# A two-layer state-space and attention trunk: the last state-space round to the end in order of use, the norm multiplied in with the scale, forget gates in steps between the value tiles, heads' loads on SyncE's queue

## The chip, the cores and the metric

The kernel runs on one core of one Trainium2 chip. The core has a matmul engine (PE, with weight loads PEld), a vector engine (DVE), an activation engine (ACT), a general engine (POOL) and SyncE (SP), which here only issues DMAs. Each engine works through its own row of instructions in order and waits on semaphores for the others; a DMA that POOL or SP issues stands in that engine's row too. The metric is device time in microseconds (us), the median of the runs. A profile of one execution, with a trace of every instruction, comes with it.

## The reference

One sequence of 1024 tokens, width 1024, passes two layers, all in float32. Shift, scale and gate of each sub-layer come from a conditioning vector c.

```python
h = _rms(x, a_norm_g) * (1 + scale) + shift            # layer 0: S5
u, z = split(h @ w_in, 2)
s = linear_scan(u)                                      # 64 groups of 16, 64 complex states
y = gelu(C @ s + D * u)
y = y * sigmoid(y @ w_glu + b_glu) * silu(z)
x = x + gate * (y @ w_out)

h = _rms(x, kv_g) * (1 + scale) + shift                 # shared keys, values, forget gates
k, v, f = split(h @ kv_w)
k = _head_rms(k, k_g);  F = cumsum(log_sigmoid(f + f_bias))

h = _rms(x, b_g) * (1 + scale) + shift                  # layer 1: attention with decay
q, z = split(h @ w_in, 2);  q = _head_rms(q, q_g) / 8
p = softmax(q @ k.T + F_i - F_j, causal)
x = x + gate * (((p @ v) * silu(z)) @ w_out)
```

## The kernel before

Every matrix product is computed from a high and a low part of both factors: `act[0]`, `act[1]` (tiles aH, aL) and `w_hi`, `w_lo`, in three matmuls (high by high, low by high, high by low). ACT makes the high part by a copy, DVE (now and then POOL) the low part by a subtraction. `weight_strip` (L83) loads 128 columns of a weight into the only `w_raw` buffer and splits them. The activations lie with the features on partitions; the 1024 tokens are two halves of 512.

The stages, with the time where each begins in the profile:

- 0 to 295 us: projections u and z, and the S5 rounds e = 0 to 7. PE's steps of a round are interleaved by hand with matmuls of the z strips, of 512, 256 or 258 columns, which `unit(n)` hands out. The last round calls `unit(2)` (L699) before `states_out`, which reads the scanned and rotated states r (L639); `unit(99)` hands out the rest.
- 295 to 387: GLU. For tile (e, i), `zt` and `yt` are loaded, `project` (L113) makes 24 matmuls into one of the two PSUM buffers of pool `pj`, and ACT's sigmoid `sg` (L772) reads it.
- 387 to 488: the out projection, 16 tiles in the order OUT_SEQ: (6,0), (7,0), (6,1), (7,1), (4,1), (5,1) are the last. Each ends in x1 = x + gate * y (L796, DVE), a store of x1 by POOL, a square (ACT) and a sum of squares (L804, POOL). After the last tile of a half, matmuls with ones give the mean, and `neg2_rsqrt` (L163) makes q2x from it: ACT Identity, Ln, Exp, then three operations of DVE.
- Norm and modulation for keys and values (L831 to 835): x1 is multiplied by q2x in place, even k on DVE and odd k on POOL, then `modulated` (L172) scales and shifts on ACT (aH) and DVE (hmod) and subtracts (aL).
- to 810: six jobs of token tiles, v0, v2, k0, k2, q0, q2 (L932). A token tile is 24 matmuls (tkps, L861) of 128 tokens by 256 columns, 272 in v0, into one of three PSUM buffers of pool `psa`. A job takes, for each half i, two strips d of four tiles. A value tile is split into vt and stored by SP; v0 also copies the forget gates' columns to flog (L875). A key or query tile goes ACT hsq (L885), DVE reduce hms (L886), POOL hms (L887, L888), DVE hnt (L890); four hnt are transposed on PE into trps (L897), split to kh and kl and stored by SP. `forget_gates` stands between v0 and v2. The second layer's activations (`modulated` with s_b, sh_b, L944) stand before q0 in the program and may be issued once k0 is done.
- 810 to 1132: attention, 64 steps of two query blocks; scores are made LOOK = 2 steps ahead. `head` (L989) loads a head's kk, qs, q and vhl, two buffers each. Between steps PE is handed matmuls of the z strips (zb) and of the first rows of the final projection (f), Z_STEP items a step, Z_END in the last.
- 1132 to the end: the other rows of the final projection (pj_f).

Between them, 64 products with the modulation weights ("gemv", modw, L131) run on DVE; `mod_load` (L136) issues the load of the next, and `mod_take` (L145) the product.

What sets the order: the framework schedules with a timing model of its own, engine by engine, in which `tc.issue_after(x)` adds an edge. What it decides is the fixed row of each engine.

```python
Q.dma_start(...)   # SP's row        G.dma_start(...)   # POOL's row
T = PE, V = DVE, S = ACT, G = POOL
```

Of the kernel before, what the change touches and what calls it, by code (L numbers as in the profile page):

```python
# [20 lines left out]
P = 128  # L21
# [16 lines left out]
F_ROWS, Z_END = 2, 2  # L38
# [7 lines left out]
def trunk(tc, a, out):  # L46
# [3 lines left out]
    with top:  # L50
# [30 lines left out]

        def weight_strip(src, shape, l_eng=None, pool=None):
            raw = (pool or wpool).tile(shape, F32, name="w_raw", tag="w_raw", bufs=2 if pool else 1)  # L83
            Q.dma_start(out=raw, in_=src)
            hi = wpool.tile(shape, F32R, name="w_hi", tag="w_hi")
            lo = wpool.tile(shape, F32R, name="w_lo", tag="w_lo")
            split(raw, hi, lo, None, l_eng)
            return hi, lo

        def copy_on(eng, o, i):  # L90
            if eng is S:
                S.activation(o, i, AF.Copy)  # L92
# [5 lines left out]
        def split(x, hi, lo, h_eng=None, l_eng=None):  # L98
            copy_on(h_eng or S, hi, x)
            (l_eng or V).tensor_tensor(out=lo, in0=x, in1=hi.bitcast(F32), op=ALU.subtract)  # L100
# [7 lines left out]
        def project_part(ps, w, act, half, ks, k0=0, k1=KT - 1):  # L108
            for k in ks:
                for n, (wt, at) in enumerate(((0, 0), (0, 1), (1, 0))):  # L110
                    T.matmul(ps, w[wt][:, k, :], act[at][k][half], start=(k == k0 and n == 0), stop=(k == k1 and n == 2))  # L111

        def project(w, act, half, nm):  # L113
            ps = pj.tile([P, HL], F32, name="pj_" + nm, tag="pj")
            project_part(ps, w, act, half, range(KT))
            return ps
# [19 lines left out]
        def mod_load(behind):  # L136
            n = mod_next[0]
            if n < 64:
# [24 lines left out]
        def neg2_rsqrt(v, r, ps, o):  # L163
            S.activation(v, ps, AF.Identity, bias=eps_t)
            S.activation(r, v, AF.Ln)
            S.activation(r, r, AF.Exp, scale=-0.5)
            V.tensor_tensor(out=v, in0=v, in1=r, op=ALU.mult)
# [4 lines left out]
        def modulated(x, k, i, s, sh, act, pool=None, l_eng=None):  # L172
            sl = slice(HL * i, HL * i + HL)
            h = pool.tile([P, HL], F32, name="hmod", tag="hmod", bufs=2) if pool else x[k][:, sl]
            S.activation(act[0][k][i], x[k][:, sl], AF.Identity, scale=s[:, k:k + 1], bias=sh[:, k:k + 1])
            V.tensor_scalar(out=h, in0=x[k][:, sl], scalar1=s[:, k:k + 1], scalar2=sh[:, k:k + 1], op0=ALU.mult, op1=ALU.add)
            (l_eng or V).tensor_tensor(out=act[1][k][i], in0=h, in1=act[0][k][i].bitcast(F32), op=ALU.subtract)  # L177
# [14 lines left out]
        with l0:  # L192
# [487 lines left out]
            for e in range(KT):  # L680
# [17 lines left out]
                if e % 2 == 0 or not more:  # L698
                    unit(1 if more else 2)  # L699
# [41 lines left out]
        x1 = [xnp.tile([P, L], F32, name=f"x1_{k}", tag=f"x1_{k}") for k in range(KT)]  # L741
        l0b = ExitStack()
        wvx = ExitStack()
        with l0b:
# [6 lines left out]
            yt = [yp.tile([P, TC, NCH], F32, name=f"yt{k}", tag=f"yt{k}") for k in range(KT)]  # L751
            for e, i in [(e, i) for e in range(KT - 2) for i in range(2)] + [(e, i) for i in range(2) for e in (KT - 2, KT - 1)]:
# [6 lines left out]
                with tc.issue_after(last_y):  # L759
                    last_q = Q.dma_start(out=zt, in_=z_d[P * e:P * e + P, i]).ins  # L760
                    if i == 0:
                        last_q = Q.dma_start(out=yt[e], in_=y_rows(e)).ins
# [7 lines left out]
                if e:  # L770
                    ps = project(wg[e], act, i, f"g{e}_{i}")
# [10 lines left out]
            psa = top.enter_context(tc.tile_pool(name="psa", bufs=3, space=PSUM, side="right", reuse_waits="tile"))  # L782
            psb = top.enter_context(tc.tile_pool(name="psb", bufs=3, space=PSUM, side="right", reuse_waits="tile"))
            gate_a = mod_bias(16, 24, "gate_a")
            held, acc, seen = {}, [None] * 2, [0, 0]
            for e, i in OUT_SEQ:
                sl = slice(HL * i, HL * i + HL)
                if e not in held:
                    if len(held) == 2:
                        del held[min(held, key=lambda n: held[n][0])]  # L790
                    held[e] = (len(seen) + sum(seen), weight_strip(a["a_w_out"][e], [P, KT, P], V, wk))
                xr = wk.tile([P, HL], F32, name="xr", tag="zt2")
                xd = Q.dma_start(out=xr, in_=a["xT"][:, e, sl]).ins
                mod_load(xd)
                ps = project(held[e][1], act, i, f"o{e}_{i}")
                mod_take(V.scalar_tensor_tensor(out=kj(x1[e][:, sl]), in0=jk(ps), scalar=gate_a[:, e:e + 1], in1=kj(xr),  # L796
                                                op0=ALU.mult, op1=ALU.add).ins, 2)
# [7 lines left out]
                else:  # L805
# [3 lines left out]
                    mps = pj.tile([P, HL], F32, name=f"ms1_{i}", tag="pj")  # L809
                    T.matmul(mps, onesm, acc[i], start=True, stop=False)  # L810
                    T.matmul(mps, onesm, sq, start=False, stop=True)
# [427 lines left out]
```

## Time and profile before

| what | us |
|---|---|
| median of 3 runs | 1207.44 (1205.32 to 1210.37) |
| the profiled execution | 1206.17 |
| its span in the trace | 1204.4 |
| PE busy / weight loads | 1153.0 / 1020.9 |
| DVE / ACT / POOL busy | 854.5 / 606.3 / 376.0 |

The profile is of one execution. "Idle before, releaser" is the time an engine stood before an instruction, and the instruction whose end let it go on. In the rows of the timeline the columns are start, duration, engine, line, operation, output <- inputs, shapes, count, and in brackets the idle time before. A q behind an engine's name marks its queue of DMAs. The granted clock is the share of PE's full clock that the throttle let through.

The costliest group of PE is the token tiles' matmul, and that of DVE the split of the transposed probabilities:

```profile
L861 PE MATMUL tkps<-wvh,aH 128*128 128x256 f32 (+1 forms) x768 | 220.6, 288 | 5.5 <-DVE flog L875 4.8
...
L1068 DVE TENSOR_TENSOR ptl<-tp,pth 128x512 fp32r<-128x512 f32 (+1 forms) x192 | 101.2, 552 | 10.6 <-ACT pth L1067 10.1
```

Such a row has the group's count, its busy time in us, the mean of one in ns, and the idle time ahead of it.

### The profile page before, as it was taken

Reading aid. Unit: us, or ns where it says so; the run is one execution under the profiler, and the core shown is the slowest. Engines: PE = TensorE matmul, PEld = TensorE weight load, DVE = VectorE, ACT = ScalarE, POOL = GpSimd, SP = SyncE. Lnnn points to the kernel's source line nnn. Section 1 sums busy time; section 2 is a strip of 40 time slices with the busy share of each in tenths; the row PEclk is TensorE's granted clock in tenths of the full one; section 3 lists DMA queues with packets and bytes.
Section 4 is the critical chain, followed back from the end, with each engine's and each line's share of the span. In section 5 each row is a group of like instructions: output and inputs, shape, how many; then the busy total and the mean of one; then the engine's idle time right before and its main releaser. Section 6 shows DMA issues by size and latency. Waiting matters only on the chain.

```text
span 1204.4 us, 20401 instructions
## 1 busy us (share of the span) xinstructions
PE 1153.0 (96%) x7414; PEld 1020.9 (85%) x7414; DVE 854.5 (71%) x1725; ACT 606.3 (50%) x1140; POOL 376.0 (31%) x586
## 2 busy tenths in 40 slices
PE   8989998997999998899999999999999999999898
PEld 6879887886788786889999989998888898888686
DVE  7889899885399877875444664347888788887421
ACT  6666766665335234322223443237677777885310
POOL 4000000000000234510044483437576665764100
PEclk9999999998999999999999999999999999999999
DMA  9754556584976894467524275527696978951342
GB/s 359 222 175 128 164 167 163 158 218 151 328 231 192 281 324 140 148 190 248 179 74 173 106 143 165 131 84 151 102 157 112 136 118 112 155 92 27 100 162 79
DMA packets 110388, 197.09 MB, mean 164 GB/s; under 512 B 17136, under 2 KB 58224, under 8 KB 108752
## 3 DMA queue, kind: packets, MB, share of 16 engines
q1 hardware_dynamic: 83072, 153.25, 40.3%
q0 software_dynamic: 25216, 37.76, 19.4%
q10 hardware_dynamic: 2000, 4.79, 1.6%
q8 instruction: 59, 0.97, 0.4%
q14 instruction: 41, 0.34, 0.1%
HBM read 138.21 MB, written 46.27 MB: 153 GB/s over the span
## 4 chain that ended last, share of the span: by engine, by line
PE 67%; DVE 13%; ACT 8%; DMA 4%; issue 4%; POOL 2%; SPq 1%; ACTq 0%; POOLq 0%; DVEq 0%
PE tkps L861 17%; PE u L274 7%; PE pj_o L111 6%; PE pj_f L111 6%; PE zb L111 5%; PE pj_g L111 5%; PE tp L1065 4%; PE ov L1072 3%; PE ov L1071 3%; PE sp L1033 2%; PE sp L1034 2%; PE z L274 2%; DVE r L207 1%; DVE w_lo L100 1%; PE f L111 1%
## 5 line engine op out<-in xcount | busy, mean ns | idle before, releaser
L861 PE MATMUL tkps<-wvh,aH 128*128 128x256 f32 (+1 forms) x768 | 220.6, 288 | 5.5 <-DVE flog L875 4.8
L861 PE MATMUL tkps<-wvl,aH 128*128 128x256 f32 (+1 forms) x768 | 217.3, 284 | 0.0
L861 PE MATMUL tkps<-wvh,aL 128*128 128x256 f32 (+1 forms) x768 | 217.0, 283 | 0.2 <-POOL aL L177 0.2
L861 PEld LDWEIGHTS tkps<-wvh,aH 128*128 128x128 f32 x768 | 145.9, 190 | 6.9 <-issue 5.4
L861 PEld LDWEIGHTS tkps<-wvl,aH 128*128 128x128 f32 x768 | 146.0, 190 | 0.3 <-issue 0.2
L861 PEld LDWEIGHTS tkps<-wvh,aL 128*128 128x128 f32 x768 | 145.5, 190 | 0.7 <-POOL aL L177 0.4
L1067 ACT ACTIVATE pth<-tp 128x512 fp32r<-128x512 f32 (+1 forms) x192 | 87.0, 488 | 56.8 <-PE ov L1071 30.6
L1040 ACT ACTIVATE pr<-pr,mx 128x128 f32<-128x128 f32 (+7 forms) x128 | 98.8, 773 | 22.6 <-DVE mx L1037 21.1
L1042 POOL TENSOR_SCALAR pr<-pr,sm 128x128 f32<-128x128 f32 (+7 forms) x128 | 95.9, 758 | 43.5 <-DVE sm L1041 41.5
L1068 DVE TENSOR_TENSOR ptl<-tp,pth 128x512 fp32r<-128x512 f32 (+1 forms) x192 | 101.2, 552 | 10.6 <-ACT pth L1067 10.1
L92 ACT ACTIVATE w_hi<-w_raw 128x1024 fp32r<-128x1024 f32 x49 | 51.6, 1054 | 90.5 <-PE pj_f L111 29.1
L1037 DVE CUSTOM_DVE_ANT_0 pr<-sp,msk 128x512 f32<-128x512 f32 (+3 forms) x128 | 72.7, 569 | 23.8 <-PE tp L1065 21.0
L1071 PE MATMUL ov<-pth,vhl 128*128 128x256 f32 x320 | 85.8, 300 | 0.2
L1065 PE MATMUL tp<-ident,pr 128*128 128x128 f32 x576 | 84.2, 275 | 1.1 <-DVE ptl L1068 1.0
L885 ACT ACTIVATE hsq<-tkps 128x256 f32<-128x256 f32 x64 | 24.5, 383 | 116.2 <-PE tkps L861 111.0
L1072 PE MATMUL ov<-ptl,vhl 128*128 128x256 f32 x320 | 81.0, 286 | 0.2
L1065 PEld LDWEIGHTS tp<-ident,pr 128*128 128x128 f32 x576 | 69.3, 141 | 11.5 <-DVE ptl L1068 2.7
L1033 PE MATMUL sp<-kk,qs 128*128 128x256 f32 (+2 forms) x192 | 71.5, 375 | 2.8 <-DVE mx L1037 2.4
L888 POOL TENSOR_TENSOR hms<-hms,nhalf 128x4 f32<-128x4 f32 x64 | 68.7, 1074 | 5.0
L890 DVE TENSOR_TENSOR hnt<-tkps,hms 128x256 f32<-128x256 f32 x64 | 27.0, 422 | 60.2 <-POOL hms L888 60.1
L1034 PE MATMUL sp<-kk,q 66*128 66x256 f32 (+2 forms) x192 | 66.2, 348 | 0.0
L887 POOL TENSOR_SCALAR hms<-hms 128x4 f32<-128x4 f32 x64 | 13.0, 203 | 165.2 <-DVE hms L886 164.1
(328 smaller groups left out, 3264.0 us busy)
## 6 DMA issues: line engine op xcount, KB each, us to landing
modw<-modw SPq DMA_DIRECT2D x48, 512.0 KB
wvr<-kvq_w SPq DMA_DIRECT2D x12, 1024.0 KB
mwx<-modw SPq DMA_DIRECT2D x16, 512.0 KB
w_raw<-a_w_in SPq DMA_DIRECT2D x16, 512.0 KB
v_d<-vt SPq DMA_DIRECT2D x32, 256.0 KB
kk<-k_d POOLq DMA_DIRECT2D x16, 512.0 KB, 7.6
vhl<-v_d POOLq DMA_DIRECT2D x16, 512.0 KB, 8.6
qs<-q_d POOLq DMA_DIRECT2D x32, 256.0 KB, 5.1
```

Of the source, the lines that this page charges most:

```text
L111: T.matmul(ps, w[wt][:, k, :], act[at][k][half], start=(k == k0 and n == 0), stop=(k == k1 and n == 2))
L274: m = T.matmul(ps[:, 0:c1 - c0], w[wt][:, k, :], act[at][k][i][:, c0:c1], start=(k == 0 and n == 0), stop=(k == KT - 1 and n == 2)).ins
L861: T.matmul(ps[:, 0:nv], at, wt[:, k, 0:nv], start=(n == 0), stop=(n == 3 * KT - 1))
L1033: T.matmul(sp[:, 0:wm_], qsl, kk[:, 0, lo:lo + wm_], start=True, stop=False)
L1034: T.matmul(sp[:, 0:wm_], q1_[:, P * i:P * i + P], kk[0:HD + 2, 1, lo:lo + wm_], start=False, stop=True)
L1040: S.activation(pr[:, 0:nk], pr[:, 0:nk], AF.Exp, scale=-1.0, bias=mx, accum_out=sm)
L1042: G.tensor_scalar(out=pr[:, 0:nk], in0=pr[:, 0:nk], scalar1=sm, scalar2=0.0, op0=ALU.mult, op1=ALU.add)
L1065: T.transpose(out=tp[:, b, :], in_=prs[qi][:, P * (b0 + b):P * (b0 + b) + P], identity=ident)
L1067: S.activation(pth[:, 0:m, dst], tp[:, 0:m, :], AF.Copy)
L1068: V.tensor_tensor(out=ptl[:, 0:m, dst], in0=tp[:, 0:m, :], in1=pth[:, 0:m, dst].bitcast(F32), op=ALU.subtract)
L1071: T.matmul(ov, vhl[:, b, :], pth[:, b - b0, :], start=(b == 0), stop=False)
L1072: end = T.matmul(ov, vhl[:, b, :], ptl[:, b - b0, :], start=False, stop=(b == nb - 1)).ins
```

## The change

1. The last S5 round calls `unit(3)`.
2. GLU and out tiles take their PSUM buffers from `psa` (three), which is opened earlier; the loads of zt and yt are chained in order of use.
3. `mod_load` stops at the 40th product until v2; the other 24 are loaded and taken in v2, k0 and k2. `mod_take` in the out stage keeps one held.
4. `neg2_rsqrt` has no Identity pass. `modulated` multiplies x1 by scale and q2x in one operation (DVE), adds the shift on ACT (aH) and in the subtraction (aL, DVE). The passes on x1 of L834 go, and POOL's share of the low parts. The mean of half 0 is put between the halves of the next out tile; half 1 of the keys' and values' modulation is put between the tiles of v0.
5. Value stores move from SP to POOL; vt takes the buffers of kh and kl. The forget gates are a generator, advanced between the tiles of v2.
6. The z strips' generator stands ahead of the jobs, and its first eight items are issued in q2's last half.
7. `head` issues all loads on SP.
8. F_ROWS is 3 and Z_END 4; row 2's strip wf2 lies in a buffer of kk.

```diff
-F_ROWS, Z_END = 2, 2
+F_ROWS, Z_END = 3, 4
...
-        def project(w, act, half, nm):
-            ps = pj.tile([P, HL], F32, name="pj_" + nm, tag="pj")
-            project_part(ps, w, act, half, range(KT))
+        def project(w, act, half, nm, pool=None, tag="pj", between=None):
+            ps = (pool or pj).tile([P, HL], F32, name="pj_" + nm, tag=tag)
+            m = project_part(ps, w, act, half, range(KT // 2))
+            if between:
+                with tc.issue_after(m):
+                    m = between()
+                with tc.issue_after(m):
+                    project_part(ps, w, act, half, range(KT // 2, KT))
+            else:
+                project_part(ps, w, act, half, range(KT // 2, KT))
             return ps
...
-        def mod_load(behind):
+        def mod_load(behind, end=5 * KT):
             n = mod_next[0]
-            if n < 64:
+            if n < end:
...
         def neg2_rsqrt(v, r, ps, o):
-            S.activation(v, ps, AF.Identity, bias=eps_t)
-            S.activation(r, v, AF.Ln)
+            S.activation(r, ps, AF.Ln, bias=eps_t)
             S.activation(r, r, AF.Exp, scale=-0.5)
-            V.tensor_tensor(out=v, in0=v, in1=r, op=ALU.mult)
+            V.scalar_tensor_tensor(out=v, in0=ps, scalar=EPS, in1=r, op0=ALU.add, op1=ALU.mult)
...
-        def modulated(x, k, i, s, sh, act, pool=None, l_eng=None):
+        def modulated(x, k, i, s, sh, act, pool=None):
...
-            S.activation(act[0][k][i], x[k][:, sl], AF.Identity, scale=s[:, k:k + 1], bias=sh[:, k:k + 1])
-            V.tensor_scalar(out=h, in0=x[k][:, sl], scalar1=s[:, k:k + 1], scalar2=sh[:, k:k + 1], op0=ALU.mult, op1=ALU.add)
-            (l_eng or V).tensor_tensor(out=act[1][k][i], in0=h, in1=act[0][k][i].bitcast(F32), op=ALU.subtract)
+            V.scalar_tensor_tensor(out=h, in0=x[k][:, sl], scalar=s[:, k:k + 1], in1=q2[:, sl], op0=ALU.mult, op1=ALU.mult)
+            S.activation(act[0][k][i], h, AF.Identity, bias=sh[:, k:k + 1])
+            V.scalar_tensor_tensor(out=act[1][k][i], in0=h, scalar=sh[:, k:k + 1], in1=act[0][k][i].bitcast(F32),
+                                   op0=ALU.add, op1=ALU.subtract)
...
-                    unit(1 if more else 2)
+                    unit(1 if more else 3)
...
-                    ps = project(wg[e], act, i, f"g{e}_{i}")
+                    ps = project(wg[e], act, i, f"g{e}_{i}", psa, "psa")
...
-                ps = project(held[e][1], act, i, f"o{e}_{i}")
+                ps = project(held[e][1], act, i, f"o{e}_{i}", psa, "psa", pending)
+                pending = None
...
-            for i in range(2):
-                sl = slice(HL * i, HL * i + HL)
-                for k in range(KT):
-                    (G if k % 2 else V).tensor_tensor(out=x1[k][:, sl], in0=x1[k][:, sl], in1=q2[:, sl], op=ALU.mult)
-                    modulated(x1, k, i, s_kv, sh_kv, act, xnp, G if k % 3 == 1 else V)
+            for k in range(KT):
+                with tc.issue_after(last_part):
+                    modulated(x1, k, 0, s_kv, sh_kv, act, xnp)
...
-                Q.dma_start(out=v_d[P * t:P * t + P, 4 * qd:4 * qd + 4, :], in_=vt.rearrange("p h a d -> p h (a d)").bitcast(F32))
+                G.dma_start(out=v_d[P * t:P * t + P, 4 * qd:4 * qd + 4, :], in_=vt.rearrange("p h a d -> p h (a d)").bitcast(F32))
...
                         for k in range(KT):
                             with tc.issue_after(k0_end):
-                                modulated(x1, k, i, s_b, sh_b, act, None, G if k % 3 == 1 else V)
+                                modulated(x1, k, i, s_b, sh_b, act)
...
+                                if job == "v0" and i == 0 and 2 <= n < 6:
+                                    for k in (2 * n - 4, 2 * n - 3):
+                                        with tc.issue_after(end):
+                                            modulated(x1, k, 1, s_kv, sh_kv, act, xnp)
+                                elif job == "v2" and t % 2:
+                                    with tc.issue_after(end):
+                                        next(gates, None)
...
-            G.dma_start(out=kk[0:HD], in_=k_d[:, rows, :].rearrange("a d t -> d a t"))
-            G.dma_start(out=kk[HD:P, 0], in_=k_d[0, rows, :])
+            Q.dma_start(out=kk[0:HD].bitcast(F32), in_=k_d[:, rows, :].rearrange("a d t -> d a t"))
+            Q.dma_start(out=kk[HD:P, 0].bitcast(F32), in_=k_d[0, rows, :])
...
-                G.dma_start(out=qs[HD * r:HD * r + HD], in_=q_d[r, rows, :])
+                Q.dma_start(out=qs[HD * r:HD * r + HD].bitcast(F32), in_=q_d[r, rows, :])
...
-            G.dma_start(out=vhl, in_=v_d[:, n, :].rearrange("(t p) f -> p t f", p=P))
+            Q.dma_start(out=vhl.bitcast(F32), in_=v_d[:, n, :].rearrange("(t p) f -> p t f", p=P))
```

Three places show how instructions stand in the engines' rows. The first is DVE's row around the norm of half 0, before (rv1 and rr1 are the norm's parts, pj_o7_1 the out tile (7,1), w_lo the low part of the next out strip):

```order
L100 TENSOR_TENSOR w_lo_4376<-w_raw_4373,w_hi_4375 128x1024
L167 TENSOR_TENSOR rv1_4295<-rv1_4295,rr1_4296 128x512
L168 TENSOR_TENSOR rv1_4295<-rv1_4295,rr1_4296 128x512
L169 SCALAR_TENSOR_TENSOR q2x_148<-rv1_4295,rr1_4296 128x512
L834 TENSOR_TENSOR x1_0_3126<-x1_0_3126,q2x_148 128x512
L834 TENSOR_TENSOR x1_2_3128<-x1_2_3128,q2x_148 128x512
L834 TENSOR_TENSOR x1_4_3130<-x1_4_3130,q2x_148 128x512
L834 TENSOR_TENSOR x1_6_3132<-x1_6_3132,q2x_148 128x512
L796 SCALAR_TENSOR_TENSOR x1_7_3133<-pj_o7_1_4342,gate_a_3824,xr_4338 128x8x64
L131 ISA modw_4259,mod_89<-modw_4259,c_b_84 128x1024
L131 ISA mod_89 128x1
L176 TENSOR_SCALAR hmod_4514<-x1_0_3126,s_kv_4475,sh_kv_4479 128x512
```

And the same place after:

```order
L176 SCALAR_TENSOR_TENSOR rv1_4298<-ms1_0_4295,rr1_4299 128x512
L177 TENSOR_TENSOR rv1_4298<-rv1_4298,rr1_4299 128x512
L810 SCALAR_TENSOR_TENSOR x1_6_3130<-pj_o6_1_4282,gate_a_3822,xr_4280 128x8x64
L178 SCALAR_TENSOR_TENSOR q2x_148<-rv1_4298,rr1_4299 128x512
L102 TENSOR_TENSOR w_lo_4357<-w_raw_4354,w_hi_4356 128x1024
L810 SCALAR_TENSOR_TENSOR x1_7_3131<-pj_o7_1_4324,gate_a_3822,xr_4322 128x8x64
L102 TENSOR_TENSOR w_lo_4395<-w_raw_4392,w_hi_4394 128x1024
L184 SCALAR_TENSOR_TENSOR hmod_4487<-x1_0_3124,s_kv_4449,q2x_148 128x512
L184 SCALAR_TENSOR_TENSOR hmod_4491<-x1_1_3125,s_kv_4449,q2x_148 128x512
L186 SCALAR_TENSOR_TENSOR aL0_0_4471<-hmod_4487,sh_kv_4453,aH0_0_4455 128x512
```

The four products of L834 and the gemvs are out of the row, both strips' w_lo stand ahead of the first hmod, and x1 of tile (7,1) comes between them.

The second is DVE's row in job k2, before. hsq, hms and hnt belong to a key tile tkps; x1 and aL of L176 and L177 are the second layer's:

```order
L886 TENSOR_REDUCE hms_6531<-hsq_6530 128x4
L176 TENSOR_SCALAR x1_0_3126<-x1_0_3126,s_b_6902,sh_b_6906 128x512
L177 TENSOR_TENSOR aL0_0_6927<-x1_0_3126,aH0_0_6911 128x512
L176 TENSOR_SCALAR x1_1_3127<-x1_1_3127,s_b_6902,sh_b_6906 128x512
L890 TENSOR_TENSOR hnt_6536<-tkps_6505,hms_6531 128x256
L176 TENSOR_SCALAR x1_2_3128<-x1_2_3128,s_b_6902,sh_b_6906 128x512
L176 TENSOR_SCALAR x1_3_3129<-x1_3_3129,s_b_6902,sh_b_6906 128x512
L177 TENSOR_TENSOR aL2_0_6931<-x1_2_3128,aH2_0_6915 128x512
```

And after, where tkps_6400 is the first tile of the second strip in half 0:

```order
L904 TENSOR_REDUCE hms_6426<-hsq_6425 128x4
L163 TENSOR_TENSOR s_b_6882<-mod_89,vecs_83 128x8
L168 SCALAR_TENSOR_TENSOR s_b_6882<-s_b_6882,vecs_83 128x8
L169 TENSOR_SCALAR s_b_6882<-s_b_6882 128x8
L184 SCALAR_TENSOR_TENSOR x1_0_3124<-x1_0_3124,s_b_6882,q2x_148 128x512
L184 SCALAR_TENSOR_TENSOR x1_1_3125<-x1_1_3125,s_b_6882,q2x_148 128x512
L184 SCALAR_TENSOR_TENSOR x1_2_3126<-x1_2_3126,s_b_6882,q2x_148 128x512
L184 SCALAR_TENSOR_TENSOR x1_3_3127<-x1_3_3127,s_b_6882,q2x_148 128x512
```

Seven more products of L184 follow in the same way (k = 4 to 7 of half 0, then 0 to 2 of half 1), and then hnt_6431, which reads tkps_6400, then two more products. In the old row the products stand singly or in pairs among the key tiles' operations.

The third is POOL's row in job q2, before (the qs loads of the first two heads among the query tiles' powers):

```order
L887 TENSOR_SCALAR hms<-hms 128x4
L888 TENSOR_TENSOR hms<-hms,nhalf 128x4
L997 DMA qs<-q_d 64x1024 x2
L887 TENSOR_SCALAR hms<-hms 128x4
L997 DMA qs<-q_d 64x1024 x2
L888 TENSOR_TENSOR hms<-hms,nhalf 128x4
```

After, they stand in SP's row, between the last strip of the token tiles' weights and q2's stores:

```order
L859 DMA wvr<-kvq_w 128x2048
L923 DMA q_d<-kh 128x512 x2
L923 DMA q_d<-kl 128x512 x2
L1052 DMA qs<-q_d 64x1024
L1053 DMA q_0_8291<-q_d 64x1024
L1052 DMA qs<-q_d 64x1024 x3
L1053 DMA q_1_8292<-q_d 64x1024
L923 DMA q_d<-kh 128x512 x2
L923 DMA q_d<-kl 128x512 x2
```

POOL's row has no load of a head left; SP's holds them together.

104 lines of the change are left out of this document (68 added, 36 removed).

## The prediction

> **What bounds the kernel now.** First the page's head and its slices:
>
> ```profile
> span 1204.4 us, 20401 instructions
> ...
> PE 1153.0 (96%) x7414; PEld 1020.9 (85%) x7414; DVE 854.5 (71%) x1725; ACT 606.3 (50%) x1140; POOL 376.0 (31%) x586
> ...
> PEclk9999999998999999999999999999999999999999
> ```
>
> PE is busy 96% of the span, and both programs issue the same matmuls, so the change can win only PE's idle time and time at a reduced clock. Next, whom PE waits for (total, times, longest), and busy time by stretch:
>
> ```profile
> PE py L639 <- DVE r L207: 8.2, 3, 6.9
> ...
> PE tkps L861 <- DVE flog L875: 4.8, 3, 1.8
> PE pj_o L111 <- DVE w_lo L100: 4.1, 2, 3.0
> PE trps L897 <- DVE hnt L890: 3.2, 3, 2.7
> ...
> PE pj_g L111 <- ACT sg L772: 2.3, 1, 2.3
> PE pj_o L111 <- DVE x L796: 1.8, 2, 1.4
> PE f L111 <- ACT aH L92: 1.7, 2, 1.1
> ...
> PE f L111 <- DVE oc L1078: 1.0, 2, 0.8
> ```
> ```profile
> 475.00:482.00 7.00, 2.61 (x12) 1.76 (x11) 7.00 (x9) 4.77 (x7) 4.72 (x5) 0.90 0.42 129
> 482.00:530.00 48.00, 42.73 (x296) 39.26 (x295) 42.59 (x67) 16.05 (x28) 23.12 (x16) 0.96 0.50 156
> ...
> 650.00:675.00 25.00, 25.00 (x193) 23.88 (x191) 16.01 (x29) 9.40 (x17) 13.04 (x18) 1.00 0.12 47
> ...
> 752.00:765.00 13.00, 10.29 (x75) 10.09 (x74) 4.31 (x6) 2.94 (x4) 7.04 (x10) 0.87 0.78 162
> ...
> 820.00:1119.00 299.00, 296.03 (x1912) 262.78 (x1911) 244.44 (x763) 222.54 (x523) 190.18 (x335) 1.00 0.73 113
> ```
>
> Columns of the second view: window, length, busy time (instructions) of PE, weight loads, DVE, ACT, POOL, then PE's granted clock, DMA share, GB/s. The losses sit in a few places. Between 475 and 530 us PE idles 9.7 of 55 us while DVE is busy 49.6: DVE bounds that stretch. Around 757 PE idles 2.7 with every engine lightly loaded: something waits on a queue. From 650 to 675 and through attention (820 to 1119) PE is nearly full, and nothing is to be won.
>
> **The last state-space round (more z matmuls ahead of the wait).**
>
> ```profile
> 258.13 1.22 DVE L100 TENSOR_TENSOR w_lo<-w_raw,w_hi 128x1024 fp32r<-128x1024 f32 x1
> ...
> 268.52 0.39 PE L274 MATMUL z<-aH,w_lo 128*128 128x512 f32 x1
> 268.75 0.28 PE L274 MATMUL z<-aH,w_hi 128*128 128x256 f32 x1
> 268.87 0.28 PE L274 MATMUL z<-aL,w_hi 128*128 128x256 f32 x1
> ...
> 276.43 1.23 DVE L207 TENSOR_TENSOR sT<-sT,v 128x1024 f32<-128x1024 f32 x1 [5.46 <-DMA v<-v]
> ...
> 279.06 0.77 PE L639 MATMUL py<-r,moa 128*128 128x128 f32 x2 [6.87 <-DVE r L207]
> ```
>
> Starts follow each other by 0.23 us at 512 columns and 0.12 at 256. PE's 6.87 us end with DVE's r, which waits for a DMA. The new order puts one more z chunk of 24 matmuls before that wait: 24 x 0.12 = 2.9 us that now run after it. Their weights are split by 259.4 us (the row of w_lo). The DMA chain is untouched. **-2.9**; the bounds are 0, if the chunk's place is lost, and -4.4, if the shorter idle also spares one slow-clock window (1.5, below).
>
> **GLU and out tiles with three PSUM buffers, fewer gemvs.**
>
> ```profile
> 331.25 0.50 PE L111 MATMUL pj_g<-aH,w_hi 128*128 128x512 f32 x1 [2.27 <-ACT sg L772]
> ...
> 408.77 1.21 DVE L131 CUSTOM_DVE_ANT_0 modw<-modw,c_b 128x1024 f32<-128x1024 f32 x1
> ...
> 411.18 0.50 PE L111 MATMUL pj_o<-aH,w_lo 128*128 128x512 f32 x1 [1.09 <-DVE w_lo L100]
> ```
>
> At 331.25 PE waits for sg to free one of two buffers; a third gives a whole tile, 24 x 0.23 = 5.6 us, of cover: **-2.3**. Ahead of the late w_lo stands a gemv of 1.21 us, one of the eight that leave the out stage; w_lo was 1.09 late: **-1.1**. Eight more leave v0; these 16 go to k0 and k2, where PE is full and DVE has a third of its time free (16 of 25 us). Bounds of the two: 0, if another of DVE's rows is late in their place, and -3.4.
>
> **Norm and modulation (475 to 530).**
>
> ```profile
> 465.91 2.30 DVE L100 TENSOR_TENSOR w_lo<-w_raw,w_hi 128x1024 fp32r<-128x1024 f32 x1
> ...
> 470.30 5.82 DVE L834 TENSOR_TENSOR x<-x,q2x 128x512 f32<-128x512 f32 x4
> ```
> ```profile
> 470.35 6.91 POOL L834 TENSOR_TENSOR x<-x,q2x 128x512 f32<-128x512 f32 x4 [3.21 <-DVE q2x L169]
> ```
>
> The norm pass is 4 operations on DVE at 1.46 us each beside 4 on POOL; w_lo takes 2.30 us here and 1.22 at 258. Only after that pass does DVE reach the next x, a gemv and w_lo, for which PE waits 1.4 and 3.0. The change takes out: this pass, 5.8 us; the gemvs between these out tiles, 1.2 each; one slot in DVE's row for the w_lo of the next strip, which now directly follows q2. The products move into modulated, one operation for one. PE's waits here: 4.8 (flog) + 3.0 + 1.4 and 0.5 of smaller = 9.7 us, and two slow-clock windows at 1.5 = 3.0. What stays: q2 still precedes the strip's w_lo, which I allow the old 1.4, and one wait of 0.7 for a token tile's buffer behind the aL row. 12.7 - 2.1: **-10.6**. Bounds: -5, if DVE's row still runs behind PE for half of it, and -12.7.
>
> [...]
>
> **Heads' loads on SyncE.**
>
> ```profile
> 754.61 1.17 POOL L997 DMA_DIRECT2D qs<-q_d  x2 [4.29 <-DMA q_d<-kh]
> ...
> 759.91 0.44 PE L897 MATMUL trps<-ident,hnt 128*128 128x128 f32 x2 [2.71 <-DVE hnt L890]
> ```
> ```profile
> 760.50:764.00 3.50, 3.50 (x19) 3.50 (x19) 0.85 (x2) 0.00 (x0) 1.46 (x3) 0.51 0.79 125
> 764.00:768.00 4.00, 4.00 (x36) 4.00 (x36) 1.74 (x3) 1.75 (x4) 0.74 (x2) 1.00 0.47 183
> ```
>
> POOL stood 4.29 us before issuing a head's load of q; the tile's hms queued behind it, then hnt, then PE. Without loads in POOL's row the 2.71 us go. The clock row shows more: 19 matmuls in 3.5 us at clock 0.51, where 36 in 4.0 make 31.5 at full clock, so 12.5 x 0.12 = 1.5 us were lost. **-4.2**. SP now waits in POOL's stead. Behind its waiting load stand only stores and loads that are due a tile later; in attention a buffer comes free a head before its load is needed, some 19 us (16 heads in 299). Bounds: 0 and -4.2; the rival below has the other sign.
>
> [...]
>
> **The end.** F's waits, 1.7 and 1.0, come when fill runs out before the last step's output passes ACT, DVE and POOL. Row 2's first half becomes fill: 24 x 0.23 = 5.6 us of matmuls, above the longest chain there (2.7 over two waits). **-2.7**, bounds -1 and -3.6 (0.9 more on pj_f).
>
> **A new wait: the second modulation, in k2.** The order of DVE after the change has reduce, three small operations, eleven products x1 in a row, and only then the hnt that frees the PSUM buffer of the fourth tile. In the old order at most three rows stand between a reduce and its hnt.
>
> ```profile
> 646.15 1.40 DVE L902 SCALAR_TENSOR_TENSOR kl<-trps,vecs,kh 128x512 fp32r<-128x512 f32 x2
> ...
> 660.70 0.42 DVE L886 TENSOR_REDUCE hms<-hsq 128x4 f32<-128x256 f32 x1
> ...
> 662.67 0.54 DVE L176 TENSOR_SCALAR x<-x,s_b,sh_b 128x512 f32<-128x512 f32 x1
> 663.13 0.41 DVE L890 TENSOR_TENSOR hnt<-tkps,hms 128x256 f32<-128x256 f32 x1
> 663.47 1.93 DVE L176 TENSOR_SCALAR x<-x,s_b,sh_b 128x512 f32<-128x512 f32 x2
> ```
> ```profile
> 660.28 0.38 ACT L885 ACTIVATE hsq<-tkps 128x256 f32<-128x256 f32 x1 [2.43 <-PE tkps L861]
> ```
> ```profile
> L288 DVE SCALAR_TENSOR_TENSOR s_a<-mod,sc,ga 128x1 f32<-128x1 f32 x8 | 1.7, 214 | 0.0
> ```
>
> From the first tile's start: 24 x 0.12 = 2.8 to its end, 0.8 for square (0.38) and reduce (0.42) with 0.1 between, 0.6 for the small ones (three at s_a's 0.2), 11 x 0.66 (kl's spacing for the same kind) = 7.3, hnt 0.4: 12.0. PE has done three tiles and two transpose pairs by 9.0: it waits 3.0. One product beside POOL's power costs 0.9 (two took 1.93 where they'd take 1.0): 0.9 more. Then hnt is followed by five products, two kl, two reduces and aL0 (5 x 0.66, 1.4, 0.8, 0.7), 6.2 us in all, while PE has one tile, two transposes and z's first matmul, 3.3: it waits 2.9. **+6.9**. Nothing in the program waits for these products to be early, so the bounds are 0, if the operations before them come so late that PE is never ahead, and +9.9 with two slow-clock windows.
>
> **The sum**, against the profiled run's 1206.17 us (median shown 1207.44, 1.3 higher): -2.9 - 2.3 - 1.1 - 10.6 - 4.2 - 2.7 + 6.9 = -16.9, so 1189.3.
>
> **The rivals.**
> - *The burst costs nothing*: 1182.4. For: the window 650 to 675 has DVE at 16 of 25. Against: the order alone makes hnt wait for eleven operations.
> - *DVE still bounds norm to v*: only 5 of 10.6 won, 1194.9. For: DVE's 42.6 of 48 busy. Against: 5.8 of pass and the gemvs are out.
> - *The slow clock isn't set by the gaps*: without three windows of 1.5, 1193.8. Against: the dips follow the gaps in the rows.
> ```profile
> kk<-k_d POOLq DMA_DIRECT2D x16, 512.0 KB, 7.6
> ```
> - *The other side: SP's single row makes heads late.* One w_raw strip that waits for its only buffer holds each head's loads behind it. From a hold above about 10 us (19 less kk's 7.6 to landing, the last number of its row) each further us delays attention by 1 us per head; 2 us at 14 heads is +28: 1217. For: twice as many transfers in one row. Against: the strips' waits lie a whole head before the slots come free.
> - *The scheduler gives it back*: orders elsewhere drift so that half of the gain is lost, 1197.7.
>
> **How the numbers follow.** 0.45 for the forecast, 0.16 burst harmless, 0.17 DVE still bound, 0.06 clock, 0.06 heads late, 0.10 given back. Half a per cent, about what a measurement tells from no change, is 6 us: faster means below 1201.4. The first four cases and most of the last do that: 0.88; 0.07 same; 0.05 slower. The range runs from 1179 (burst harmless, larger bounds) to 1199 (given back): it leaves out the heads' case and the far ends of the terms.
>
> **What would show it.** Right: no idle before pj_g at 331; pj_o and flog waits between 455 and 530 at 1 to 3 us in all; no hnt wait near 757 and a clock of 1.00 behind it; an idle stretch of about 3 to 4 us before tkps on hnt in k2 and another before zb; f's waits gone. Wrong: new waits on kk, qs or vhl DMAs in attention, or sp idle above the 3.0 us of 820 to 1119.

## The result and the profile after

The changed kernel takes 1196.1 us (median of 4 runs, 1194.45 to 1198.09) against 1208.61 of the kernel before (4 runs, 1205.32 to 1210.37). The ratio is 0.990, with a 95% interval from 0.9871 to 0.9929. The profiled execution took 1195.09 us, its span is 1193.3; before, these were 1206.17 and 1204.4.

The head of the page after, and PE's clock by slices:

```profile
span 1193.3 us, 20366 instructions
...
PE 1149.9 (96%) x7414; PEld 1018.9 (85%) x7414; DVE 854.7 (72%) x1729; ACT 603.7 (51%) x1136; POOL 315.3 (26%) x518
...
PEclk8999999999999999999999999999999999999999
```

POOL has 61 us less to do; DVE has as much as before, in another order. The waits of PE in the changed kernel (total, times, longest; line numbers are the changed kernel's):

```profile
PE pk L589 <- DVE moa L217: 6.5, 7, 1.7
PE py L649 <- DVE r L217: 5.3, 3, 4.0
PE pin L577 <- DVE wm L217: 3.7, 3, 2.8
PE msx L308 <- ACT sqx L306: 3.6, 2, 2.6
PE tkps L879 <- DVE hnt L908: 3.1, 1, 3.1
PE tkps L879 <- ACT aH L185: 2.7, 2, 1.5
...
PE ov L1112 <- DVE ptl L1108: 1.7, 1, 1.7
...
PE pj_o L113 <- ACT w_hi L94: 1.1, 1, 1.1
PE zb L113 <- DVE aL L186: 0.9, 1, 0.9
```

Against the list of before: py on r has shrunk, pj_g on sg, trps on hnt and f on aH are gone, f on oc is down to 0.2, and nearly all waits of tkps on flog and of pj_o on w_lo and x are gone. Grown are pin on wm (in the first 125 us, 0.9 before) and tkps on hnt (in k2, 0.5 before); new are tkps on aH (in v0), pj_o on w_hi, zb on aL (in k2) and ov on ptl (in attention). The stretches, in the columns of the prediction's second view:

```profile
475.00:482.00 7.00, 7.00 (x36) 5.76 (x34) 7.00 (x8) 3.38 (x5) 3.38 (x3) 1.00 0.25 75
482.00:530.00 48.00, 44.86 (x350) 42.97 (x350) 31.42 (x52) 17.98 (x31) 11.72 (x18) 1.00 0.28 102
...
640.00:662.00 22.00, 18.01 (x123) 16.79 (x122) 20.29 (x37) 8.00 (x15) 6.77 (x9) 0.92 0.35 128
662.00:752.00 90.00, 90.00 (x713) 87.16 (x711) 53.97 (x98) 32.34 (x54) 41.08 (x55) 1.00 0.55 173
752.00:800.00 48.00, 47.21 (x398) 46.58 (x398) 20.23 (x48) 11.85 (x28) 19.62 (x33) 1.00 0.32 106
```

From 475 to 530 PE idles 3.1 us (before 9.7), and its clock is never lowered there. From 640 to 662 it idles 4.0 where before it was full (busy 22.00 of 22.00 us at a clock of 1.00), and the clock falls to 0.92 in the mean.

To put all of it in one sum: for each two neighbouring matmuls of PE the time from start to start, less the median of its shape, is time lost (a wait or a slow clock). Added up by stretch, from the two traces (the forecast column has the terms of the prediction's sum):

| stretch, us | lost before | lost after | change | forecast |
|---|---|---|---|---|
| tables, norm, first u (0 to 125) | 20.7 | 25.6 | +4.9 | 0 |
| S5 rounds (125 to 300) | 27.2 | 24.8 | -2.4 | -2.9 |
| GLU, out tiles (300 to 450) | 3.6 | 0.5 | -3.1 | -3.4 |
| norm, v (450 to 625) | 18.7 | 8.2 | -10.5 | -10.6 |
| k0, k2 (625 to 700) | 0.0 | 6.1 | +6.1 | +6.9 |
| q0, q2 (700 to 775) | 5.4 | 0.0 | -5.4 | -4.2 |
| attention starts (775 to 825) | 5.4 | 5.0 | -0.4 | 0 |
| attention (825 to 1100) | 7.3 | 9.1 | +1.8 | 0 |
| end (from 1100) | 5.7 | 2.9 | -2.8 | -2.7 |
| sum | 94.0 | 82.2 | -11.8 | -16.9 |

The forecast has 5.1 us too much. The first and the eighth row make 6.7, a stage that it did not look at and one that it called full; the other rows came out 1.6 better.

### The profile page after: what moved, and what is told of

The parts are those of the page before. It is cut to its first block, busy times and chain, and to the rows that moved or that the text cites. A ratio compares the mean times of both kernels' runs of the same rounds, so it can differ in the third digit from the quotient of the medians.

```text
span 1193.3 us, 20366 instructions
## 1 busy us (share of the span) xinstructions
PE 1149.9 (96%) x7414; PEld 1018.9 (85%) x7414; DVE 854.7 (72%) x1729; ACT 603.7 (51%) x1136; POOL 315.3 (26%) x518
## 4 chain that ended last, share of the span: by engine, by line
PE 74%; DVE 12%; ACT 7%; DMA 3%; issue 3%; ACTq 0%; SPq 0%; DVEq 0%
PE tkps L879 22%; PE pj_g L113 7%; PE zb L113 6%; PE pj_f L113 5%; PE u L284 5%; PE pj_o L113 5%; PE tp L1105 4%; PE ov L1111 3%; PE ov L1112 3%; PE sp L1073 2%; PE f L113 2%; PE sp L1074 2%; PE z L284 2%; PE msx L308 1%; ACT pr L1080 1%
## 5 line engine op out<-in xcount | busy, mean ns | idle before, releaser
L1080 ACT ACTIVATE pr<-pr,mx 128x128 f32<-128x128 f32 (+7 forms) x128 | 98.8, 773 | 24.1 <-DVE mx L1077 22.5
L1108 DVE TENSOR_TENSOR ptl<-tp,pth 128x512 fp32r<-128x512 f32 (+1 forms) x192 | 101.1, 552 | 10.6 <-ACT pth L1107 10.2
L1105 PEld LDWEIGHTS tp<-ident,pr 128*128 128x128 f32 x576 | 69.0, 141 | 13.2 <-DVE ptl L1108 4.5
L1111 PEld LDWEIGHTS ov<-pth,vhl 128*128 128x128 f32 x320 | 61.0, 191 | 3.2 <-DVE oc L1118 2.0
L1112 PEld LDWEIGHTS ov<-ptl,vhl 128*128 128x128 f32 x320 | 61.2, 191 | 3.0 <-DVE ptl L1108 3.0
```

The lines of the kernel that those rows point to most:

```text
L1080: S.activation(pr[:, 0:nk], pr[:, 0:nk], AF.Exp, scale=-1.0, bias=mx, accum_out=sm)
L1105: T.transpose(out=tp[:, b, :], in_=prs[qi][:, P * (b0 + b):P * (b0 + b) + P], identity=ident)
L1108: V.tensor_tensor(out=ptl[:, 0:m, dst], in0=tp[:, 0:m, :], in1=pth[:, 0:m, dst].bitcast(F32), op=ALU.subtract)
L1111: T.matmul(ov, vhl[:, b, :], pth[:, b - b0, :], start=(b == 0), stop=False)
L1112: end = T.matmul(ov, vhl[:, b, :], ptl[:, b - b0, :], start=False, stop=(b == nb - 1)).ins
```

## The experiments

Each is an edit of the changed kernel, or of the kernel before where that is said. Times are medians; the ratio is to the kernel before on the same chip. "Lost" is the sum of the table above. The changed kernel's 1196.1 us (ratio 0.990) was not timed side by side with the experiments. The kernel before took 1208.6 beside it and 1206.1 to 1208.3 beside them, so a difference of 2 or 3 us to the changed kernel counts only where the ratio shows it too.

### Where the first 125 us come from

The function `neg2_rsqrt` also serves the first layer's norm. In ACT's row before, the sine of the tables (ang, behind a load of its function table) stood here:

```profile
59.82 1.28 ACT L397 ACT_TABLE_LOAD   x1
61.12 0.26 ACT L397 ACTIVATE ang<-th 128x64 f32<-128x64 f32 x1
```

After the change it comes 5.5 us later, DVE's powers follow it, and PE waits for wm:

```profile
65.30 1.28 ACT L407 ACT_TABLE_LOAD   x1
66.59 0.26 ACT L407 ACTIVATE ang<-th 128x64 f32<-128x64 f32 x1
...
86.44 0.72 PE L577 MATMUL pin<-ident,wm 128*128 128x128 f32 x4 [2.84 <-DVE wm L217]
```

*old_norm0* gives the first norm its old chain (`neg2_rsqrt0`, a copy of the old function):

```diff
...
-                neg2_rsqrt(vx[:, sl], q2[:, sl], mps[i], q2[:, sl])
+                neg2_rsqrt0(vx[:, sl], q2[:, sl], mps[i], q2[:, sl])
```

> The changed kernel with the old neg2_rsqrt (Identity pass first) for the first norm only; the kv norm keeps the short one. Theory: the prologue's 4.9 us of lost PE time (PE's excess over its start-to-start times, 0 to 125 us: 20.7 before, 25.6 after) come from the short norm, which also serves the first layer and moved the sine of the tables behind other rows of ACT. Then the wait of pin on wm (2.8 us at 83.6) is gone, the wait of u on bi (3.2 us near 63) is back, and the time is 4 to 5 us below the changed kernel's 1196.1: 1191 to 1192. Rival: the prologue of that one execution was slow by chance (loads at the start); then the time stays within 1 us of 1196.

Measured: 1193.68 us (1191.87 to 1196.42), ratio 0.989 (0.9867 to 0.9913). The wait of pin on wm is gone and that of u on bi is back, as expected:

```profile
PE u L293 <- DVE et L352: 2.8, 1, 2.8
...
PE u L293 <- DVE bi L366: 1.9, 1, 1.9
```

But the stretch lost 23.1 us here, where the same row of instructions lost 20.7 in the profile of before: u on et, 2.8, had no place there. ACT's row stood 5.13 us for the load of x1m, where it stood 2.21 in the profile of before, and DVE's ang and et come behind ACT; so a later landing made that wait, not the order. The time is 2.4 lower, half of what was expected, and the ratio's interval lies over the changed kernel's: the time alone does not show the gain.

*before_norm* puts the short chain alone into the kernel before:

```diff
-            S.activation(v, ps, AF.Identity, bias=eps_t)
-            S.activation(r, v, AF.Ln)
+            S.activation(r, ps, AF.Ln, bias=eps_t)
...
-            V.tensor_tensor(out=v, in0=v, in1=r, op=ALU.mult)
+            V.scalar_tensor_tensor(out=v, in0=ps, scalar=EPS, in1=r, op0=ALU.add, op1=ALU.mult)
```

> The kernel before with the short neg2_rsqrt alone (both norms), everything else as before. Theory: the prologue's new wait appears here too: pin on wm near 2.8 us, PE's excess from 0 to 125 us near 25.6 in place of 20.7; the kv norm's shorter chain gains at most 1, so 1208.6 + 4 to 5 = 1212 to 1214. Rival (the slow prologue was chance): 1207 to 1209.

Measured: 1211.58 us (10 runs, 1209.27 to 1216.99) against 1206.4, ratio 1.0044 (1.0023 to 1.0064): slower by 5.2 us, with the new wait in the place foretold:

```profile
PE pin L566 <- DVE wm L206: 2.8, 1, 2.8
```

Its first 125 us lost 27.8, in a profile of the slowest of the ten runs, and 450 to 550 us lost 17.8, as before the change (17.9): the shorter chain by itself gained nothing at the second norm. Over all profiles of this study the first 125 us lost 25.7 in the mean with the short first norm (8 kernels, 23.7 to 27.8) and 22.7 with the old one (6 kernels, 20.7 to 24.1). So the short chain costs some 3 us there; the other 2 of the 4.9 are the luck of one profile, since that of before has the least of the six.

### The burst of products in k2

DVE's row in k2 after the change, and PE behind it:

```profile
643.84 0.41 DVE L904 TENSOR_REDUCE hms<-hsq 128x4 f32<-128x256 f32 x1
...
644.79 7.38 DVE L184 SCALAR_TENSOR_TENSOR x<-x,s_b,q2x 128x512 f32<-128x512 f32 x11
652.09 0.42 DVE L908 TENSOR_TENSOR hnt<-tkps,hms 128x256 f32<-128x256 f32 x1
```
```profile
652.56 0.39 PE L879 MATMUL tkps<-wvh,aH 128*128 128x256 f32 x1 [3.12 <-DVE hnt L908]
```

Eleven products took 7.38 us (7.3 was worked out), and PE waited 3.12. The prediction had 3.0 for this wait and 0.9 more for a product beside POOL's power; here no product was slowed (0.67 us each), and the power beside them took 1.01 us. *spread* ties the products to the tiles of the second strip, two behind each:

```diff
-                            with tc.issue_after(k0_end):
+                            with tc.issue_after(last_nt[20 + 8 * i + k // 2]):
```

> The changed kernel with the second modulation's products tied to the key tiles of k2, two behind each tile of the second strip, in place of all behind k0. Theory: the row of eleven products ahead of one hnt makes the waits in k2 (tkps on hnt 3.1, zb on aL 0.9) and the slow-clock window at 653.5. Then these three go, 5 to 6 us in all: 1190 to 1191. Rival: it is the amount of DVE's work there, and the waits only move to other tiles: no more than 2 us gained, 1194 or more.

Measured: 1193.38 us (1190.07 to 1196.79), ratio 0.9893 (0.9866 to 0.992). The lost time of 625 to 700 us falls from 6.1 to 2.1: the wait on hnt is gone, and zb waits twice, 0.8 at most and 1.4 in all:

```profile
PE zb L113 <- DVE aL L186: 1.4, 2, 0.8
```

The 0.7 us of lost time that is left is less than the 1.5 us at which the prediction estimated one slow stretch of the clock. So the row, not DVE's amount of work, made the cost; 4 us of it went from the stretch, not 5 to 6. The time is 2.7 lower, which the ratio does not tell from no change.

*both* has the two edits together.

> Both edits together. If the two costs are separate, the gains add: 9 to 11 us below the changed kernel, 1185 to 1187, ratio to the kernel before 0.981. If one hides behind the other, about 1191.

Measured: 1188.1 us (1186.81 to 1190.86), ratio 0.9852 (0.983 to 0.9874). That is 8.0 below the changed kernel and more than either alone, though short of 9 to 11; by the ratio the two intervals still touch. In its trace each stretch falls as it does alone (the first 125 us lose 22.2, k0 and k2 lose 2.0), so neither cost hides behind the other.

### What the norm stage's gain is made of

*before_pass* puts the new `modulated` into the kernel before and takes the passes out, with norm, gemvs and buffers as they were (the code of the new `modulated` is that of the change):

```diff
...
-                    (G if k % 2 else V).tensor_tensor(out=x1[k][:, sl], in0=x1[k][:, sl], in1=q2[:, sl], op=ALU.mult)
-                    modulated(x1, k, i, s_kv, sh_kv, act, xnp, G if k % 3 == 1 else V)
+                    modulated(x1, k, i, s_kv, sh_kv, act, xnp)
```

> The kernel before with the new modulated alone: the passes of L834 and POOL's share of the low parts are gone, the norm, the gemvs, the buffers and the order of the stages stay as before. Theory (the pass is the larger part of the norm stage's 10.6): PE's excess from 450 to 550 us falls from 17.9 by 6 to 8, the wait on w_lo of 3.0 is gone; the second modulation's burst of products appears in k2 (+4 to 6). Time near 1206. Rival (the gemvs and the order carry it): the norm stage gains under 3, time 1208 or more.

Measured: 1210.43 us, ratio 1.0024 (0.9999 to 1.005). The lost time of 450 to 550 us fell from 17.9 to 13.2, and k2 lost 5.5 in its place. PE's waits from 450 to 550:

```profile
PE tkps L861 <- DVE aL L177: 3.1, 2, 2.3
PE tkps L861 <- DVE flog L875: 3.0, 1, 3.0
PE pj_o L111 <- DVE x L797: 0.4, 1, 0.4
```

The wait on w_lo went, the token tiles' did not: the pass, with POOL's share of the low parts, is worth 4.7, less than the 6 to 8 expected, and alone it is paid back in k2. The time came out 4.2 above the kernel before's 1206.2 and not near 1206; the profile also lost 3.4 more in the first 125 us and 2.4 more in the S5 rounds, which the edit does not touch.

*gemvs* goes the other way, and puts the modulation products back where they were:

```diff
-        def mod_load(behind, end=5 * KT):
+        def mod_load(behind, end=8 * KT):
...
-                                                op0=ALU.mult, op1=ALU.add).ins, max(0, min(2, len(mod_held) - 1)))
+                                                op0=ALU.mult, op1=ALU.add).ins, 2)
...
-                            if t % 2 and job != "v0":
+                            if t % 2:
```

> The changed kernel with the modulation products loaded and taken where they were before: 16 in the out stage, none held back for k0 and k2. Theory: of the norm stage's gain 2 to 4 come from these 1.2 us pieces of DVE's row, so pj_o and tkps waits from 400 to 550 rise by 2 to 4 over the changed kernel's; s_b is ready long before k2, so the burst of products starts earlier and may stand elsewhere. Rival: they lie beside PE's work and return nothing (under 1).

Measured: 1202.16 us (8 runs), ratio 0.9963 (0.995 to 0.9976), 6 us slower than the changed kernel. From 450 to 550 us it lost 12.3, 4.6 more. The burst in k2 stayed (5.4 lost). So the gemvs are worth as much as the pass; the two make 9.3 of the 10.2 that the changed kernel saves from 450 to 550 us. One was added to the old kernel and the other taken out of the new one, so that they add up is not itself shown; the stores on POOL and the forget gates in steps were not undone singly, though tkps still waits 3.0 on flog in *before_pass* and 0.4 in the changed kernel.

### The three PSUM buffers, the order of the loads, and the z chunk

*pj2_unit2* undoes two edits in places far apart:

```diff
-                    unit(1 if more else 3)
+                    unit(1 if more else 2)
...
-                    ps = project(wg[e], act, i, f"g{e}_{i}", psa, "psa")
+                    ps = project(wg[e], act, i, f"g{e}_{i}")
...
-                ps = project(held[e][1], act, i, f"o{e}_{i}", psa, "psa", pending)
+                ps = project(held[e][1], act, i, f"o{e}_{i}", between=pending)
```

> The changed kernel with two edits undone that lie far apart: unit(2) in the last S5 round, and GLU and out tiles in pj's two buffers. Theory: the idle before the last round's py rises by 2.9 (one z chunk), and pj_g's wait of 2.3 on sg is back; the waits of the norm stage rise by no more than 1. Rival for the first: the idle follows the landing of the swapped states, which differs from run to run by as much (4.0 to 5.6 in three runs of the changed order), and the chunk alone shows less than 2.

Measured: 1196.62 us (2 runs), ratio 0.9925 (0.99 to 0.9949): no difference from the changed kernel. py's longest wait on r is 6.8:

```profile
PE py L649 <- DVE r L217: 8.8, 3, 6.8
```

With `unit(2)` four kernels show 6.8 to 7.3, with `unit(3)` ten show 2.5 to 6.3, 4.7 in the mean: a difference of 2.3 in the means, and one pair of profiles could have shown anything from 0.5 to 4.8. The spread is the transfer's: DVE stood for the swapped states between 4.0 and 7.5 us in these profiles (5.46 before the change, 5.32 in the changed kernel). PE's wait was 1.4 to 1.7 longer than DVE's in all four kernels with `unit(2)`, and 1.2 to 1.6 shorter in all ten with `unit(3)`. So at the same landing the chunk is worth 3.0.

But pj_g did not wait: two buffers are enough. From 450 to 550 us this kernel lost 5.8, less than the changed one (7.7); the wait of pj_o on w_hi is not there. From 300 to 450 us it lost 1.6 in place of 0.5, with pj_o 1.25 on w_lo at 398, so the two buffers themselves return little.

*unchain* keeps three buffers and takes the chain of loads away, so that SP's row has loads of yt ahead of zt again:

```diff
-                with tc.issue_after(last_q):
+                with tc.issue_after(last_y):
                     last_q = Q.dma_start(out=zt, in_=z_d[P * e:P * e + P, i]).ins
                     if i == 0:
-                        with tc.issue_after(last_q):
-                            last_q = Q.dma_start(out=yt[e], in_=y_rows(e)).ins
+                        last_q = Q.dma_start(out=yt[e], in_=y_rows(e)).ins
```

> The changed kernel with the loads of zt and yt as before (not chained; SP's row has yt loads ahead of zt again), but with three PSUM buffers for the GLU tiles. Theory: the late load of zt, with ACT's row waiting behind it, made the wait of pj_g on sg; the third buffer only hides it. With two buffers and chained loads there was no wait; if here there is none either, each of the two edits is enough alone, and the wait of 2.3 is nowhere. Rival: the order of the loads alone decides, and 2 us of wait on sg are back between 300 and 350 us.

Measured: 1196.91 us (2 runs), ratio 0.9901 (0.9862 to 0.994), and no wait of pj_g either. Each of the two edits removes the wait alone. In the profile of before, the load of zt was what DVE stood for, 5.6 us, just ahead of that wait:

```profile
326.70 0.69 DVE L764 TENSOR_TENSOR zt<-zt,q2p 128x512 f32<-128x512 f32 x1 [5.61 <-DMA zt<-z_d]
```

In *unchain* DVE stands as long for the late load, and with three buffers PE does not wait behind it:

```profile
333.23 0.69 DVE L775 TENSOR_TENSOR zt<-zt,q2p 128x512 f32<-128x512 f32 x1 [5.62 <-DMA zt<-z_d]
```

### The heads' loads

*pool_heads* issues kk, qs and vhl on POOL again:

```diff
-            Q.dma_start(out=kk[0:HD].bitcast(F32), in_=k_d[:, rows, :].rearrange("a d t -> d a t"))
+            G.dma_start(out=kk[0:HD], in_=k_d[:, rows, :].rearrange("a d t -> d a t"))
...
-            Q.dma_start(out=vhl.bitcast(F32), in_=v_d[:, n, :].rearrange("(t p) f -> p t f", p=P))
+            G.dma_start(out=vhl, in_=v_d[:, n, :].rearrange("(t p) f -> p t f", p=P))
```

> The changed kernel with the heads' loads back on POOL's row. Theory: the wait of trps on hnt in q2 (2.7) and the slow-clock window behind it return, 4 us more between 700 and 800 us; attention unchanged within 1. Rival (SP's row costs attention what POOL's cost q2): attention, 825 to 1100, gains 2 or more in exchange.

Measured: 1201.33 us (5 runs, 1198.23 to 1203.09), ratio 0.9962 (0.9941 to 0.9982), 5 us slower than the changed kernel. From 700 to 800 us PE has two waits, 2.7 at 758 as before the change, and one of 1.7 at 715 where the kernel before had none above 0.3:

```profile
PE trps L915 <- DVE hnt L908: 4.5, 2, 2.7
```

The slow clock that followed the 2.7 before the change (0.51 from 760.5 to 764.0 us) did not come back: here the granted clock was 1.00 in the same stretch. Attention from 825 to 1100 us lost 9.1 both with POOL's and with SP's queue. SP's single row of loads cost nothing there.

### The third row of the final projection

*frows* sets F_ROWS and Z_END back, and takes out the early load of row 2's strip:

```diff
-F_ROWS, Z_END = 3, 4
+F_ROWS, Z_END = 2, 2
...
```

> The changed kernel with F_ROWS and Z_END back at 2, 2. Theory: f's waits return at the end of attention, PE's excess after 1100 us rises by 2 to 3. Rival: the extra row's strip makes waits of its own on DVE in the last steps (ov on ptl 1.7, tp on ptl 1.0), which go when it goes: a gain of 2 against a loss of 2.5, no difference.

Measured: 1197.16 us (3 runs), ratio 0.9923 (0.99 to 0.9945). The end loses 5.7 again in place of 2.9, and attention from 1025 to 1100 loses 4.8 in place of 6.4. Both theories hold: the row gains 2.8 at the end and costs 1.6 before it. The time shows no difference. In the changed kernel's DVE row the strip's split stands ahead of a ptl that PE waits for:

```profile
1076.23 1.67 DVE L102 TENSOR_TENSOR wf<-w_raw,wf 128x1024 fp32r<-128x1024 f32 x1
1077.82 0.68 DVE L1108 TENSOR_TENSOR ptl<-tp,pth 128x512 fp32r<-128x512 f32 x1
```
```profile
1078.55 0.38 PE L1112 MATMUL ov<-ptl,vhl 128*128 128x256 f32 x1 [1.68 <-DVE ptl L1108]
```

### A faster version

*both2* has the old first norm, and the products two tiles earlier than in *spread* and *both* (the diff is against *both*):

```diff
...
-                            with tc.issue_after(last_nt[20 + 8 * i + k // 2]):
+                            with tc.issue_after(last_nt[18 + 8 * i + k // 2]):
```

> Both edits together, with the second modulation's products one strip earlier (behind the last two tiles of the first strip and the first two of the second). Theory: the two waits of zb on aL that were left (1.8 us at 686 and 694) go, since aL is ready a tile earlier, and four products ahead of an hnt still fit the buffers' slack: 1186 to 1187. Rival: the earlier products make the hnt wait again, 1188 or more.

Measured: 1185.6 us (1185.42 to 1187.02), ratio 0.9835 (0.9819 to 0.9852). From 625 to 700 us it lost 0.7 (*both* 2.0).

*both3* adds what *pj2_unit2* and *frows* showed: two buffers for GLU and out tiles, and the strip of row 2 split by POOL (the diff is against *both2*):

```diff
...
-                split(raw, *wf[e])
+                split(raw, *wf[e], l_eng=G)
```

> As both2, with two more edits: GLU and out tiles in pj's two buffers, and row 2's strip split by POOL in place of DVE. Theory: the wait of ov on ptl near 1068 (1.7) stands behind the strip's w_lo on DVE and goes; the out stage's wait on w_hi (1.1) went with two buffers in another run: 1.5 to 3 below both2's 1185.6, 1183 to 1184. Rival: POOL's pr row is late instead and a wait of tp or ov takes the place; 1185 or more.

Measured: 1183.51 us (6 runs, 1182.91 to 1184.69), ratio 0.9793 (0.9769 to 0.9816). The wait of ov on ptl is gone (825 to 1100 us lost 6.9; *both2* 8.4), and so is the one of pj_o on w_hi. But pj_o waits 1.26 on w_lo at 393 (*both2* 0.65): 450 to 550 us lost 1.7 less than in *both2*, 300 to 450 us 1.5 more, so the stretches show a gain from POOL's split and next to none from the two buffers. This is the fastest of all: 12.6 us below the changed kernel, 24.8 below the kernel before that was timed beside it (1208.32).

## Why the prediction was right, and where it was not

1. **What bounds the kernel** held: the whole gain is PE idle time and slow clock, and it lies in the places named.
2. **The last round**: -2.9 forecast, -2.3 in the means of the 14 profiles, 3.0 at the same landing of the swapped states. Mechanism and size are right; the landing moves the wait by 3.5 us from run to run, so a single pair of profiles could not settle the size, and the table's -2.4 is partly chance.
3. **GLU and out tiles**: the waits went, 3.1 of 3.4. The cause given was incomplete: the step said that a third buffer gives the cover, yet with two buffers and ordered loads there is no wait either.
4. **Norm and modulation**: -10.6 forecast, -10.5 found. Two parts are of one size, 4.7 for the pass with POOL's low parts (alone, in the kernel before) and 4.6 for the gemvs (alone, taken back). What stays is 1.1 on w_hi and 2.7 on ACT's aH, not the waits that were allowed for: aH now stands behind DVE's product, and ACT ends the chain.
5. **Heads' loads**: -4.2 forecast, -5.4 in the two profiles, 4.9 when undone. The wait of 2.7 was right. The clock's 1.5 is not sure: with the loads back on POOL the same idle of 2.71 us was followed by a granted clock of 1.00 (below), and a second wait of 1.7 made up the size, so the nearness of 4.9 to 4.2 is partly luck. The rival of late heads fell.
6. **The end**: -2.7 forecast, -2.8 found; the bound did not see the price, 1.6 in attention, where the row's strip is split by DVE ahead of ptl.
7. **The new wait in k2**: +6.9 forecast, +6.1 found. The first wait was 3.12, as worked out without POOL (3.0). No run shows the 0.9 for a product beside POOL's power: in the row that it was taken from, two operations in 1.93 us at 663.47, POOL was at a subtraction (L177, 1.29 us from 663.36) and not at a power, and after the change eleven products took 7.38, 0.67 each, and the power beside them 1.01. The second wait, 2.9 forecast, was 0.9 (up to 658.50): PE ran at a clock of 0.50 from 653.5 to 656.9, with 19 matmuls in these 3.4 us, and came later to it. That slow clock, which the sum left out, cost little of its own: zb's wait ends with DVE's aL, so DVE's row sets when zb can start. Behind a first wait of 3.1 in each of them, zb did not wait in *frows* and *old_norm0* and waited 2.4 in *pj2_unit2*, so the second wait differs from run to run.
8. **What was missing**: the first 125 us, some 3 us over all profiles and 4.9 in this one. The step that failed is a term that the sum put at nothing without a reason: the edit to `neg2_rsqrt` was read as one of the second norm only. The function has two callers, and at the first one ACT has one operation fewer for each half of the tokens, after which the scheduler put other rows first. Attention, called full with nothing to be won, lost 1.8 more in the pair of profiles; 1.6 of it is the price in point 6.

Of 16.9 us forecast, 12.5 came between the medians and 11.1 between the two profiled executions. The forecast of 1189.3 was 6.8 us below the median; 2.4 of that is its start from a profiled execution faster than the median of before. The measured time lies nearer to two rivals. *DVE still bounds norm to v* (1194.9) is ruled out by its own stage, which gained 10.5. *The scheduler gives it back* (1197.7, a chance of 0.10) came true in part, some 3 us at a place that was not named.

## What to carry to other kernels

When a helper is edited, list its callers, and compare each engine's row at every one of them, also far from the place that the edit is meant for: a chain that gets shorter can still move its neighbours. Operations that have lost their last dependency (here products that once came behind ACT's aH, which waits for a buffer) are issued in one run by a scheduler; tie them to the steps between which they should stand. Undoing a part in the new kernel and doing it alone in the old one give different answers (the pass alone gained 4.7 and was paid back), so both are worth a run.

## What the runs showed of the hardware that was not expected

The same idle of PE was followed by a lowered clock in one execution and not in another. Before the change, 2.71 us of idle up to 759.91 were followed by 3.5 us at a clock of 0.51 with 19 matmuls (the prediction's row). In *pool_heads* the same wait, also 2.71 us, up to 757.78, was followed by a granted clock of 1.00 up to 764.0, with 32 matmuls in the last 3.5 us:

```profile
757.78 0.44 PE L915 MATMUL trps<-ident,hnt 128*128 128x128 f32 x2 [2.71 <-DVE hnt L908]
```
```profile
757.00:760.40 3.40, 2.62 (x22) 2.63 (x23) 1.54 (x4) 0.00 (x0) 2.66 (x5) 1.00 1.24 199
760.50:764.00 3.50, 3.50 (x32) 3.50 (x31) 1.74 (x3) 1.54 (x3) 0.41 (x2) 1.00 0.47 173
```

What tells the two executions apart was not shown. For a forecast it means that a saved wait of 2.71 us can't be counted on to save the slow clock's 1.5 us as well: it was there in one of these two profiles.
